# Differential-attention stacks read in two transfers from interleaved maps, with conditioning units, key stacks and loads of heads in other places

## The chip, the cores and the metric

The kernel runs on one core of one Trainium2 chip. The metric is the device time of one execution in microseconds (us); lower is better. In the profile the engines are called PE (TensorE, matrix products), PEld (its weight loads), DVE (VectorE), ACT (ScalarE), POOL (GpSimd) and SP (SyncE, which here issues every transfer between memory and SBUF).

## The reference: what is computed

Two layers over 512 latent tokens and 256 context tokens, model width 1024, batch 1, all in float32. A layer is a token mixer and then a gated convolutional FFN. What the change touches is the first of the mixer's four head groups, differential attention, and the conditioning vectors:

```python
mod_l = (c_act @ w_mod[l] + b_mod[l])[:, None, :]          # conditioning: 6 x 1024 values a layer
hl = modulate(rmsnorm(xl, norm_mix_w[l]), sh1, sc1) @ w_in[l]
q = h[..., :A_Q].reshape(b, s, DIFF_HEADS, 2, DIFF_QK_DIM)  # 4 heads, 2 maps, 32 channels each
s = jnp.einsum('bhiqd,bhikd->bhiqk', q, k).astype(f32) * scale
p = jax.nn.softmax(s, axis=-1)
w = (p[:, :, 0] - lam * p[:, :, 1]).astype(v.dtype)
```

Queries and keys of this group and of the second one (window attention) are turned by a rotary embedding before that.

## The kernel before

**Precision.** Every float32 operand of a product is split into a high and a low part, and products of the parts are added. For the scores of differential attention, one map has 32 channels, so a *stack* of 128 partitions holds four blocks of 32: high, high, low, low for the queries and high, low, high, low for the keys. One product over 128 partitions then gives all four combinations.

**Stages.** A head stage computes the first eight conditioning units (`mod_products`, `mod_sums`; a unit is 256 values, its weights are two loads of 512 KB into tiles `mraw`), the first norm and the first products with `w_in` while its inputs arrive. Then for each layer come the mixer, the output product and the FFN. In the mixer of layer 0, TensorE alternates between pieces of 22 projections with `w_in` (a unit `win`, 512 KB of weights into a tile `raw`, cast by ScalarE into `wh` and reduced by GpSimd to `wl`) and the attention of eight items: A0 heads 0 and 1, A1 heads 0 and 1, B heads 0 and 1, C0, C1. The remaining twelve conditioning units of layer 0 are woven in between the pieces by `side`.

**How a stack comes about.** The projection of queries or keys of a group is turned (`rotate`), split and written to memory by `stash` (tile `qk`, high and low part, 128 channels, 768 tokens). `load` of the group then reads it back as stacks with `stack`: in group A four transfers of 32 partitions each, two stacks (queries and keys) a head. All transfers are issued by SP in the order that the scheduler gives them. `begin` calls `load` at the first score of a head's first item, and for the following head at the first score of its second item (an item is two blocks of 128 queries). Stacks live in a pool `stk` of four buffers. Loads of weights run one unit ahead in layer 0 and two units ahead in layer 1, in a pool of three `raw` buffers that the conditioning weights of the mixer share.

**Order.** The program's order on each engine is what a scheduler made of the code; scores and pieces of TensorE are pinned to the order of the code. Each engine works strictly in its order.

Of the kernel before, what the change touches and what calls it, by code (L numbers as in the profile page):

```python
# [9 lines left out]
F32 = mybir.dt.float32  # L10
# [42 lines left out]
class Trunk:  # L53
# [34 lines left out]
    def build(self):  # L88
# [53 lines left out]
        for j in range(4):  # L142
            for h in (j, j + 4):
                raws = [self.g.tile([128, 2 * T], F32, tag="g", name="mraw") for _ in range(2)]
                raws = [t[:, 0:1024].rearrange("p (g n) -> p g n", g=4) for t in raws]
                for kh in range(2):
                    last = nc.sync.dma_start(out=raws[kh], in_=d["wmod"][h, kh])
                self.mod_sums(0, h, self.mod_products(h, raws, "pj" if h < 4 else "pv"))
            if j == 0:
                self.depth = 0  # L150
                self.prefetch(2)
            ks = range(2 * j, 2 * j + 2)
            self.scale_vec(0, self.amix[0], O_NM, 8, slice(2 * j, 2 * j + 2))
            for sg, rb in zip(SEGS, r):
                self.norm_apply(x, y, sg, self.amix[0], self.mod[0][:, 0:8], rb, ks)
            early = early or self.early_start(0)
            for k in ks:
                for sg in SEGS:
                    self.early_products(early, y, sg, [k])
# [10 lines left out]
        for l in range(DEPTH):  # L170
# [3 lines left out]
            with ExitStack() as es:  # L174
                self.mixing_pools(es)
                todo = []
                if l == 0:
                    todo = list(range(8, 20))
                if l:
                    self.neg_lambda(l)  # L180
                self.mixing(l, y, need, todo)
# [363 lines left out]
    def side(self, last):  # L545
        if self.open:
            self.open.pop()()
        elif self.vq:
            self.vq.pop(0)()
        elif self.todo and not last and self.mraw:  # L550
            h = self.todo.pop(0)
            parts = self.mod_products(h, self.mraw.pop(), "pv" if self.name == "A0" else "tp")
            self.open.append(lambda: self.mod_sums(0, h, parts))
        if self.todo and not self.mraw:
            self.mraw.append(self.mod_load(self.todo[0]))
# [14 lines left out]
    def rotate(self, t, kind):  # L570
        nc = self.nc
        step = 8 if kind == 0 else 16
        mask = [i ^ step for i in range(32)]
        s = self.hl.tile([128, T], F32, tag="hl", name="rot")
# [6 lines left out]
    def split(self, t, NT, vector=False, pool=False):  # L581
# [5 lines left out]
        return hl  # L587

    def stash(self, t, NT, vector=False):

        hl = self.split(t, NT, vector, self.name == "B")
        self.n += 1
        scr = self.tc.dram_tile([2, 128, T], F32, name=f"qk{self.n}")
        self.nc.sync.dma_start(out=scr[:, :, :NT].rearrange("s p t -> p s t"), in_=f32v(hl[:, :, :NT]))
        return scr

    def stack(self, pieces, NT):

        s = self.stk.tile([128, 2, T], F32R, tag="stk", name="stk")
        o = 0  # L600
# [137 lines left out]
    def mixing(self, l, y, need, todo):  # L738
        qs = SEGS if need else SEGS[:1]
        self.l, self.y, self.qs, self.NQ, self.todo = l, y, qs, T if need else SEQ, todo  # L740
        self.open, self.vq, self.later, self.mraw = [], [], [], []
        self.depth = 1 if todo else AHEAD
        self.kept = {}
        self.pairs = []
# [60 lines left out]
        def score(n):  # L805
            nonlocal at
            for _ in range(n):
                if at < len(scores):
# [5 lines left out]
                    after(w * SCORE_SHARE)  # L814

        for n, (name, _, _, ws, v_steps, fin) in enumerate(items):
            v = v_steps()
# [24 lines left out]
    def items(self, g, name, h, need_prep):  # L842
        L = list(g.attend(h))
        for i, (s_steps, ws, v_steps) in enumerate(L):
            yield (name, (lambda i=i: g.begin(h, i, need_prep)) if i in (0, 1) else None, s_steps, ws, v_steps,
                   i == len(L) - 1 and (name[0] != "A" and name[0] != "B" or h == 1))
# [128 lines left out]
class Group:  # L975
# [28 lines left out]

    def k64(self, scr, j):
        src = scr[:, 64 * j:64 * j + 64].rearrange("s d t -> d s t")
        return self.K.stack([src, src], T)


class GroupA(Group):  # L1010
# [7 lines left out]
    def prep(self):  # L1018
        K, P = self.K, self.P
        self.qscr = yield from self.qk(P, self.qs, 32 ** -0.5, 0)  # L1020
        self.kscr = yield from self.qk(2 + P, SEGS, 1.0, 0)
        K.have.add(K.name)
# [4 lines left out]
    def load(self, hh):  # L1027

        self.ops[hh] = [
            self.K.stack([scr[s, 64 * hh:64 * hh + 64, :NT].rearrange("(m d) t -> d m t", d=32) for s in parts], NT)  # L1030
            for scr, parts, NT in ((self.qscr, (0, 0, 1, 1), self.NQ), (self.kscr, (0, 1, 0, 1), T))]

# [84 lines left out]
class GroupB(Group):  # L1117
# [18 lines left out]
    def load(self, j):  # L1136
        self.ops[j] = self.k64(self.kscr, j), self.q64(self.qscr[j])

# [189 lines left out]
def _tables():  # L1328
# [4 lines left out]
    for kind, dim in ((0, 32), (1, 64)):  # L1333
        quarter = dim // 4
        freqs = (f(10000.0) ** (-(np.arange(quarter, dtype=f) / f(quarter)))).astype(f)
        for p in range(128):
            i = p % dim
            pos = rows if i < dim // 2 else cols
# [21 lines left out]
def _layout(i):  # L1360
# [8 lines left out]
    r["wmodt"] = A["w_mod"].reshape(L, D, 48, 128).transpose(0, 2, 3, 1)  # L1369
    r["win"] = A["w_in"].reshape(L, KT, 128, 22, 128).transpose(0, 3, 2, 1, 4)  # L1370
    r["wout"] = A["w_out"].reshape(L, KT, 128, KT, 128).transpose(0, 3, 2, 1, 4)
    r["wup"] = A["ffn_w_up"].reshape(L, KT, 128, 2, NF, 128).transpose(0, 4, 3, 2, 1, 5)
# [39 lines left out]
```

## Time and profile before

| | |
|---|---|
| time, median of 3 runs | 1759.32 us (1756.22 to 1762.36) |
| the profiled execution | 1762.87 us, its span 1761.0 us |
| TensorE busy | 1679.1 us, 95% of the span |
| granted clock of TensorE, mean of the span | 0.986 |
| VectorE, ScalarE, GpSimd busy | 53%, 45%, 58% |
| DMA, mean over the span | 139 GB/s |

TensorE's busy time is the sum of its products, whose ends are modelled; a stretch where it waits is a gap between two rows of its timeline, and the wait's cause stands in brackets at the later row. [...] The time of a transfer has two parts in the profile: how long SP was taken up by issuing it (its row in SP's timeline), and how long it took from issue to landing (the table of DMA issues).

### The profile page before, as it was taken

How to read it: one execution, taken by the hardware profiler on the slowest of the kernel's cores; microseconds unless marked ns; L12 is line 12 of the kernel's file. 1: busy time of each engine (PE TensorE's matmuls, PEld its weight loads, DVE VectorE, ACT ScalarE, POOL GpSimd, SP SyncE). 2: the span in 40 equal slices, each digit the busy share in tenths (PEclk: the TensorE clock that was granted, in tenths of full speed). 3: DMA queues.
4: the chain of work that ended last, by engine and by line, in shares of the span. 5: the costliest groups of instructions: out<-in, count | busy, mean ns of one | idle time of the engine just before them, and what ended most of it. 6: DMA issues, size and time to landing. Idle time of an engine off the chain costs nothing. (4 is left out here: it accounts for less than half of the span.)

```text
span 1761.0 us, 27484 instructions
## 1 busy us (share of the span) xinstructions
PE 1679.1 (95%) x10212; PEld 1448.2 (82%) x10212; DVE 928.5 (53%) x1789; ACT 787.5 (45%) x1355; POOL 1017.3 (58%) x1348
## 2 busy tenths in 40 slices
PE   7899999899999999999999988999999999999997
PEld 4578878798888888888888877888889888888887
DVE  3577767562767644543344566877656522122244
ACT  4377656553533311332133345776654543242343
POOL 1424235766678745775466664424865676676762
PEclk9999999999999999999999999999999999999998
DMA  8675545346533333343334536453436333333334
GB/s 334 177 217 188 156 115 179 93 122 231 168 108 121 124 113 98 120 131 110 119 111 135 181 113 188 138 150 102 147 109 221 106 99 90 102 93 99 96 114 127
DMA packets 78453, 244.21 MB, mean 139 GB/s; under 512 B 9072, under 2 KB 12656, under 8 KB 78192
## 3 DMA queue, kind: packets, MB, share of 16 engines
q1 hardware_dynamic: 78320, 242.46, 43.8%
q8 instruction: 81, 1.33, 0.3%
q14 instruction: 52, 0.43, 0.1%
HBM read 214.64 MB, written 27.79 MB: 138 GB/s over the span
## 5 line engine op out<-in xcount | busy, mean ns | idle before, releaser
L485 POOL TENSOR_TENSOR wl<-raw,wh 128x256 fp32r<-128x256 f32 (+1 forms) x750 | 575.2, 797 | 542.7 <-ACT wh L480 526.5
L480 ACT CAST wh<-raw 128x1024 fp32r<-128x1024 f32 (+1 forms) x228 | 233.5, 1027 | 422.7 <-PE pd L73 194.9
L73 PE MATMUL pu<-yh,wh 128*128 128x512 f32 (+1 forms) x1072 | 377.4, 352 | 1.8 <-DVE up L925 1.8
L73 PE MATMUL pu<-yl,wh 128*128 128x512 f32 (+1 forms) x1072 | 377.2, 352 | 1.8 <-POOL yl L411 1.5
L73 PE MATMUL pu<-yh,wl 128*128 128x512 f32 (+1 forms) x1072 | 376.3, 351 | 0.0
L73 PE MATMUL pd<-g,wh 128*128 128x512 f32 (+1 forms) x1168 | 290.9, 341 | 5.4 <-DVE x L893 2.4
L922 DVE SCALAR_TENSOR_TENSOR up<-pu,par,up 128x511 f32<-128x511 f32 (+1 forms) x132 | 83.0, 657 | 329.0 <-ACT up L920 329.0
L73 PEld LDWEIGHTS pd<-g,wh 128*128 128x128 f32 x1168 | 203.2, 192 | 31.1 <-ACT wh L480 5.6
L73 PEld LDWEIGHTS pu<-yh,wh 128*128 128x128 f32 x1072 | 202.7, 189 | 29.7 <-ACT wh L480 1.5
L73 PEld LDWEIGHTS pu<-yl,wh 128*128 128x128 f32 x1072 | 202.8, 189 | 29.3 <-POOL yl L411 2.1
L73 PEld LDWEIGHTS pu<-yh,wl 128*128 128x128 f32 x1072 | 202.7, 189 | 27.4
L73 PE MATMUL pj<-yh,wh 128*128 128x512 f32 (+1 forms) x608 | 217.4, 361 | 7.2 <-ACT ev L559 4.9
L73 PE MATMUL pj<-yl,wh 128*128 128x512 f32 (+1 forms) x608 | 213.6, 352 | 1.5 <-DVE yl L413 1.4
L73 PE MATMUL pj<-yh,wl 128*128 128x512 f32 (+1 forms) x608 | 212.4, 350 | 0.0
L73 PE MATMUL pd<-g,wl 128*128 128x512 f32 (+1 forms) x584 | 198.4, 341 | 4.6 <-DVE wl L485 4.5
L893 DVE SCALAR_TENSOR_TENSOR x<-pd,mod,x 128x512 f32<-128x512 f32 (+1 forms) x80 | 48.9, 614 | 181.9 <-PE pd L73 181.9
L73 PEld LDWEIGHTS pj<-yh,wh 128*128 128x128 f32 x608 | 117.1, 193 | 26.0 <-ACT ev L559 8.4
L73 PEld LDWEIGHTS pj<-yh,wl 128*128 128x128 f32 x608 | 117.2, 193 | 14.6
L655 POOL TENSOR_TENSOR p<-p,rec 128x512 f32<-128x512 f32 (+2 forms) x80 | 79.5, 997 | 85.6 <-DVE rec L651 62.6
L73 PEld LDWEIGHTS pj<-yl,wh 128*128 128x128 f32 x608 | 117.6, 193 | 13.2 <-DVE yl L413 3.1
L73 PEld LDWEIGHTS pd<-g,wl 128*128 128x128 f32 x584 | 112.3, 192 | 18.0 <-DVE wl L485 5.5
L310 DVE SCALAR_TENSOR_TENSOR junk<-mrow,cbc 128x1024 f32<-128x1024 f32 x80 | 123.2, 1541 | 1.4 <-DMA mrow<-in_wmodt 0.5
(176 smaller groups left out, 2750.5 us busy)
## 6 DMA issues: line engine op xcount, KB each, us to landing
raw<-in_wup SPq DMA_DIRECT2D x88, 512.0 KB, 3.5
mrow<-in_wmodt SPq DMA_DIRECT2D x56, 512.0 KB, 3.8
raw<-in_win SPq DMA_DIRECT2D x44, 512.0 KB, 3.7
raw<-in_wdn SPq DMA_DIRECT2D x48, 448.0 KB, 3.3
mraw<-in_wmod SPq DMA_DIRECT2D x40, 512.0 KB, 7.1
raw<-in_wout SPq DMA_DIRECT2D x32, 512.0 KB, 3.5
qk<-hl SPq DMA_DIRECT2D x16, 768.0 KB, 3.6
stk<-qk SPq DMA_DIRECT2D x32, 384.0 KB, 5.5
```

What stands on the lines that cost most here:

```text
L73: i = self.nc.tensor.matmul(out, **kw)
L310: self.tc.keep_in_program_order(nc.vector.scalar_tensor_tensor(out=junk, in0=raw, scalar=1.0, in1=self.cbc[:, i], op0=ALU.mult, op1=ALU.mu ...
L480: i = nc.scalar.copy(out=wh, in_=raw)
L485: eng.tensor_tensor(out=wl[:, a:b], in0=raw[:, a:b], in1=f32v(wh[:, a:b]), op=ALU.subtract)
L655: self.nc.gpsimd.tensor_tensor(out=p, in0=p, in1=r.broadcast_to(list(p.shape)), op=ALU.mult)
L893: self.nc.vector.scalar_tensor_tensor(out=x[m][:, a:b], in0=p[:, :b - a], scalar=gate[:, m, (0 if b <= SEQ else 1):(1 if b <= SEQ else 2)] ...
L922: nc.vector.scalar_tensor_tensor(out=u[:, a + 1:b], in0=p[:, a:b - 1], scalar=cw[:, 0:1], in1=u[:, a + 1:b], op0=ALU.mult, op1=ALU.add)
```

## The change

Eight edits:

1. The columns of `w_in` for queries and keys of group A are reordered so that the two maps' channels alternate (partition 2d + m holds channel d of map m); the table of the rotary embedding and the shuffle (distance 16 in place of 8) follow it.
2. `stash` writes into a memory tile that is as wide as its tokens, so that the two maps of one channel are one run of memory.
3. A stack of group A is read by `stack2` in two transfers of 64 partitions in place of four of 32. The queries' transfers repeat the high (or low) half with a step of 0; the keys' go over both halves.
4. Of A0's head 0 the query stack is loaded as soon as the queries are stored.
5. A0's head 1 is loaded at the third item of head 0 in place of the second (in layer 1, which has two items, still at the second), pinned to that place in SP's order; B's head 1 likewise at the third item of head 0.
6. The key stack of B's head 1 lives in the pool of the values (`vp`) in place of `stk`.
7. Conditioning units 8 and 9 move from the mixer into the head stage, into its last of four rounds.
8. In the mixer no conditioning weights are loaded and no conditioning unit starts before the first score.

The diff, cut to its core:

```diff
@@ build, head stage
+            more = []
+            if j == 3:
+                for h, tag in ((8, "pj"), (9, "pv")):
+                    raws = [self.g.tile([128, 2 * T], F32, tag="g", name="mraw") for _ in range(2)]
+                    raws = [t[:, 0:1024].rearrange("p (g n) -> p g n", g=4) for t in raws]
+                    for kh in range(2):
+                        nc.sync.dma_start(out=raws[kh], in_=d["wmod"][h, kh])
+                    more.append((h, self.mod_products(h, raws, tag)))
...
-                    todo = list(range(8, 20))
+                    todo = list(range(10, 20))
@@ side
-        elif self.todo and not last and self.mraw:
+        elif self.begun and self.todo and not last and self.mraw:
...
-        if self.todo and not self.mraw:
+        if self.begun and self.todo and not self.mraw:
@@ rotate
-        step = 8 if kind == 0 else 16
-        mask = [i ^ step for i in range(32)]
+        mask = [i ^ 16 for i in range(32)]
@@ stack2 (new), stash
+    def stack2(self, src, same, NT, late=False):
+        s = self.stk.tile([128, 2 * T], F32R, tag="stk", name="stk")
+        for i in range(2):
+            part = src[i:i + 1].broadcast_to([2, 32, 2 * NT]) if same else src
+            self.load(f32v(s[64 * i:64 * i + 64, :2 * NT]), part, late)
+        return s[:, :2 * NT].rearrange("p (m t) -> p m t", m=2)
...
-        scr = self.tc.dram_tile([2, 128, T], F32, name=f"qk{self.n}")
+        scr = self.tc.dram_tile([2, 128, NT], F32, name=f"qk{self.n}")
@@ items
+            second = min(2, len(L) - 1) if (name, h) in (("A0", 0), ("B", 0)) else 1
@@ GroupA
-        self.ops[hh] = [
-            self.K.stack([scr[s, 64 * hh:64 * hh + 64, :NT].rearrange("(m d) t -> d m t", d=32) for s in parts], NT)
-            for scr, parts, NT in ((self.qscr, (0, 0, 1, 1), self.NQ), (self.kscr, (0, 1, 0, 1), T))]
+        have = self.ops.get(hh, [])
+        self.ops[hh] = have + [self.half(hh, i) for i in range(len(have), 2)]
+
+    def half(self, hh, i):
+        scr, NT = (self.kscr, T) if i else (self.qscr, self.NQ)
+        src = scr[:, 64 * hh:64 * hh + 64].rearrange("s (d m) t -> s d (m t)", m=2)
+        return self.K.stack2(src, i == 0, NT, self.P == 0 and hh == 1)
@@ GroupB.load
+        if j:
+            assert sum(K.vlive.values()) < 4
+            K.vlive["B"] += 1
+            home = K.vp
+        self.ops[j] = self.k64(self.kscr, j, home), self.q64(self.qscr[j])
```

What the change does to SP's order shows at three places of layer 0's mixer; each row is one transfer or several equal ones, with its destination, its source and the destination's size. **First place: the start of the mixer**, from the store of A0's queries (`qk_688` before, `qk_728` after) and keys (`qk_701`, `qk_744`) to the stacks of head 0. Before:

```order
L271 DMA mraw<-in_wmod 128x1024
L594 DMA qk_688<-hl_685 128x2x768
L271 DMA mraw<-in_wmod 128x1024
L594 DMA qk_701<-hl_698 128x2x768
L603 DMA stk<-qk_688 32x2x768 x4
L271 DMA mraw<-in_wmod 128x1024 x2
L603 DMA stk<-qk_701 32x2x768 x4
L603 DMA stk<-qk_688 32x2x768 x4
```

After:

```order
L612 DMA qk_728<-hl_725 128x2x768
L612 DMA qk_744<-hl_741 128x2x768
L477 DMA raw<-in_win 128x1024
L477 DMA stk<-qk_728 64x1x1536 x2
L477 DMA stk<-qk_744 64x1x1536 x2
L281 DMA mraw<-in_wmod 128x1024
L612 DMA qk_889<-hl_886 128x2x768
```

The conditioning loads (`mraw`) are gone from among the stores and the stacks, and head 0's stacks are four transfers in place of eight; the query stack still stands behind the store of the keys. **Second place: the loads of A0's head 1 and A1's head 0.** Before, from the store of A1's keys (`qk_1100`) on; A0's head 1 had been loaded earlier, right behind head 0:

```order
L594 DMA qk_1100<-hl_1097 128x2x768
L467 DMA raw<-in_win 128x1024
L1231 DMA rpb<-in_rpb 128x384
L603 DMA stk<-qk_894 32x2x768 x4
L603 DMA stk<-qk_1100 32x2x768 x4
L467 DMA raw<-in_win 128x1024
```

After, from the store of A1's keys (`qk_1056`) on:

```order
L612 DMA qk_1056<-hl_1053 128x2x768
L477 DMA raw<-in_win 128x1024
L477 DMA stk<-qk_728 64x1x1536 x2
L477 DMA stk<-qk_744 64x1x1536 x2
L477 DMA stk<-qk_889 64x1x1536 x2
L477 DMA stk<-qk_1056 64x1x1536 x2
L1265 DMA rpb<-in_rpb 128x384
L477 DMA raw<-in_win 128x1024
```

Eight transfers of stacks, those of two heads, now stand in one row ahead of the next load of weights. **Third place: A1's head 1**, the last load of group A. Before:

```order
L594 DMA qk_1662<-hl_1659 128x2x768
L603 DMA stk<-qk_894 32x2x768 x4
L603 DMA stk<-qk_1100 32x2x768
L467 DMA raw<-in_win 128x1024
L603 DMA stk<-qk_1100 32x2x768 x3
```

After:

```order
L612 DMA qk_1624<-hl_1621 128x2x768
L477 DMA stk<-qk_889 64x1x1536 x2
L477 DMA stk<-qk_1056 64x1x1536 x2
L477 DMA raw<-in_win 128x1024
L281 DMA mraw<-in_wmod 128x1024 x2
```

The load of weights stood among the last of eight transfers and now stands behind all four.

## Rows read from the trace of the kernel before

**Rows 1.** Busy time by stage: head, layer 0's mixer, then to layer 1's mixer.

```profile
core 0: us, PE busy (x) PEld busy (x) DVE busy (x) ACT busy (x) POOL busy (x), PEclk, DMA share, GB/s
20.00:40.00 20.00, 18.09 (x156) 10.65 (x155) 12.41 (x36) 8.83 (x17) 5.53 (x8) 1.00 1.00 405
...
60.00:230.00 170.00, 157.14 (x1009) 129.15 (x1008) 118.77 (x267) 107.99 (x218) 59.61 (x65) 0.98 0.60 184
...
400.00:1060.00 660.00, 649.90 (x3827) 570.97 (x3826) 336.04 (x571) 211.74 (x262) 426.61 (x482) 0.99 0.42 131
1060.00:1185.00 125.00, 116.85 (x675) 100.92 (x674) 94.10 (x166) 84.39 (x151) 49.73 (x60) 0.97 0.53 158
```

**Rows 2.** PE's longest waits at the start of layer 0's mixer: total us, times, longest.

```profile
PE macc L73 <- DMA mraw<-in_wmod: 4.8, 2, 4.5
...
PE sca L73 <- DMA stk<-qk: 1.1, 1, 1.1
```

**Rows 3.** SP's timeline there: start us, us of issuing, line, transfer, count.

```profile
70.33 0.34 SPq L271 DMA_DIRECT2D mraw<-in_wmod  x1
70.71 0.43 SPq L594 DMA_DIRECT2D qk<-hl  x1
71.19 4.28 SPq L603 DMA_DIRECT2D stk<-qk  x4
75.57 1.09 SPq L271 DMA_DIRECT2D mraw<-in_wmod  x2
77.46 6.92 SPq L603 DMA_DIRECT2D stk<-qk  x8
```

**Rows 4.** PE's timeline there: start us, us, tile, count, wait before it.

```profile
75.52 0.74 PE L73 MATMUL macc<-mraw,silc 128*32 128x256 f32 x8 [4.53 <-DMA mraw<-in_wmod]
...
87.80 0.94 PE L73 MATMUL sca<-stk 128*128 128x512 f32 x4 [1.14 <-DMA stk<-qk]
```

**Rows 5.** Two stretches of PE just behind that wait, columns as in Rows 1.

```profile
76.20:79.20 3.00, 3.00 (x12) 2.31 (x9) 0.00 (x0) 1.31 (x2) 1.44 (x3) 0.50 1.09 252
79.60:82.60 3.00, 3.00 (x20) 2.02 (x18) 0.75 (x5) 0.30 (x1) 0.95 (x2) 1.00 1.02 352
```

**Rows 6.** DMA issues: transfer, count, KB each, median us from issue to landing.

```profile
raw<-in_win SPq DMA_DIRECT2D x44, 512.0 KB, 3.7
...
stk<-qk SPq DMA_DIRECT2D x32, 384.0 KB, 5.5
stk<-qk SPq DMA_DIRECT2D x48, 192.0 KB, 5.5
...
out<-ot SPq DMA_DIRECT2D x8, 256.0 KB, 2.1
```

**Rows 7.** PE's timeline: first scores of A0 head 1, A1 heads 0 and 1.

```profile
118.94 0.51 PE L73 MATMUL sca<-stk 128*128 128x512 f32 x2
...
155.36 0.59 PE L73 MATMUL sca<-stk 128*128 128x512 f32 x2
...
193.14 0.39 PE L73 MATMUL sca<-stk 128*128 128x512 f32 x1
```

**Rows 8.** SP's timeline: A1's key store, then three loads of weights of units.

```profile
109.49 0.38 SPq L594 DMA_DIRECT2D qk<-hl  x1
112.19 0.33 SPq L467 DMA_DIRECT2D raw<-in_win  x1
...
128.09 0.35 SPq L467 DMA_DIRECT2D raw<-in_win  x1
...
157.06 1.58 SPq L467 DMA_DIRECT2D raw<-in_win  x1
```

**Rows 9.** ACT's casts of the last two of those, PE's first products with them.

```profile
138.15 1.03 ACT L480 CAST wh<-raw 128x1024 fp32r<-128x1024 f32 x1
146.98 0.50 PE L73 MATMUL pj<-yh,wh 128*128 128x512 f32 x1
147.31 0.40 PE L73 MATMUL pj<-yl,wh 128*128 128x512 f32 x1
147.55 0.39 PE L73 MATMUL pj<-yh,wl 128*128 128x512 f32 x1
...
164.14 1.05 ACT L480 CAST wh<-raw 128x1024 fp32r<-128x1024 f32 x1
173.73 0.39 PE L73 MATMUL pj<-yh,wh 128*128 128x512 f32 x1
```

**Rows 10.** SP and PE at the start of layer 1's mixer.

```profile
1070.23 6.49 SPq L603 DMA_DIRECT2D stk<-qk  x10
...
1079.62 0.59 PE L73 MATMUL sca<-stk 128*128 128x512 f32 x2 [1.16 <-DMA stk<-qk]
...
1100.59 0.52 PE L73 MATMUL sca<-stk 128*128 128x512 f32 x2
```

**Rows 11.** PE's timeline: scores of group C that waited for stacks.

```profile
324.46 0.71 PE L73 MATMUL scc<-stk 128*128 128x256 f32 x4 [2.81 <-DMA stk<-qk]
...
1278.75 1.19 PE L73 MATMUL scc<-stk 128*128 128x256 f32 x4 [3.31 <-DMA stk<-qk]
```

More of the change, by code (lines that the diff above doesn't have):

```diff
@@ L155, in build @@
                 self.norm_apply(x, y, sg, self.amix[0], self.mod[0][:, 0:8], rb, ks)
+            for h, parts in more:
+                self.mod_sums(0, h, parts)
             early = early or self.early_start(0)
@@ L592, in stash, with stack @@
         self.n += 1
-        scr = self.tc.dram_tile([2, 128, T], F32, name=f"qk{self.n}")
-        self.nc.sync.dma_start(out=scr[:, :, :NT].rearrange("s p t -> p s t"), in_=f32v(hl[:, :, :NT]))
-        return scr
-    def stack(self, pieces, NT):
-        s = self.stk.tile([128, 2, T], F32R, tag="stk", name="stk")
+        scr = self.tc.dram_tile([2, 128, NT], F32, name=f"qk{self.n}")
+        self.nc.sync.dma_start(out=scr.rearrange("s p t -> p s t"), in_=f32v(hl[:, :, :NT]))
+        return scr
+    def stack(self, pieces, NT, home=None):
+        s = (home or self.stk).tile([128, 2, T], F32R, tag="v" if home else "stk", name="stk")
         o = 0
@@ L742, in mixing @@
         self.depth = 1 if todo else AHEAD
+        self.begun = False
         self.kept = {}
@@ L814, in score @@
                     after(w * SCORE_SHARE)
+            self.begun = self.begun or n > 0
         for n, (name, _, _, ws, v_steps, fin) in enumerate(items):
@@ L844, in items @@
         for i, (s_steps, ws, v_steps) in enumerate(L):
-            yield (name, (lambda i=i: g.begin(h, i, need_prep)) if i in (0, 1) else None, s_steps, ws, v_steps,
+            second = min(2, len(L) - 1) if (name, h) in (("A0", 0), ("B", 0)) else 1
+            yield (name, (lambda i=i: g.begin(h, i, need_prep)) if i in (0, second) else None, s_steps, ws, v_steps,
                    i == len(L) - 1 and (name[0] != "A" and name[0] != "B" or h == 1))
@@ L1003, in q64, with k64 @@
         return self.K.stack([scr[s, :, :self.NQ].rearrange("(g d) t -> d g t", d=64) for s in range(2)], self.NQ)
-    def k64(self, scr, j):
+    def k64(self, scr, j, home=None):
         src = scr[:, 64 * j:64 * j + 64].rearrange("s d t -> d s t")
-        return self.K.stack([src, src], T)
+        return self.K.stack([src, src], T, home)
 class GroupA(Group):
@@ L1020, in prep @@
         self.qscr = yield from self.qk(P, self.qs, 32 ** -0.5, 0)
+        if P == 0:
+            self.ops[0] = [self.half(0, 0)]
         self.kscr = yield from self.qk(2 + P, SEGS, 1.0, 0)
@@ L1136, in load @@
     def load(self, j):
-        self.ops[j] = self.k64(self.kscr, j), self.q64(self.qscr[j])
+        K = self.K
+        home = None
+        if j:
[3 more added lines that the diff above has]
+        self.ops[j] = self.k64(self.kscr, j, home), self.q64(self.qscr[j])
     def attend(self, j):
@@ L1336, in _tables @@
         for p in range(128):
-            i = p % dim
+            i = p % 64 // 2 if kind == 0 else p % dim
             pos = rows if i < dim // 2 else cols
@@ L1370, in _layout @@
     r["win"] = A["w_in"].reshape(L, KT, 128, 22, 128).transpose(0, 3, 2, 1, 4)
+    two = np.arange(128).reshape(2, 2, 32).transpose(0, 2, 1).reshape(128)
+    r["win"] = np.concatenate([r["win"][:, :4][..., two], r["win"][:, 4:]], axis=1)
     r["wout"] = A["w_out"].reshape(L, KT, 128, KT, 128).transpose(0, 3, 2, 1, 4)
```

## The prediction

> **What bounds the kernel now.** I read the stages first: in the FFN TensorE is busy 649.9 of 660 us, in layer 0's differential attention 157.1 of 170 and in layer 1's 116.9 of 125 [rows 1]. The change touches nothing of the FFN, so all it can save lies in these gaps; what it can lose has no such limit, since TensorE works in order and waits for whatever it needs next. I then read whom TensorE waits for where the change acts: at the start of layer 0's mixer 4.5 us for conditioning weights and 1.1 us for head 0's stacks [rows 2, 4]. SP's timeline gives the reason: the weights' load is issued at 70.33, the keys' store and four stack transfers right behind it, and SP is taken up 4.28 us by those four and 6.92 us by the next eight [rows 3]; the load lands at 75.5 among this traffic. [...] Last come group C's scores, which wait 2.81 us in layer 0 and up to 3.31 us in layer 1 for stacks that found no free buffer [rows 11].
>
> **The change part by part.**
>
> *Free edits.* The reordered columns, the rotary table and the shuffle's distance change no count and no size of an instruction. The width of the stored tile changes addresses alone.
>
> *Conditioning units.* Twenty units stay twenty; two of them move. What goes away is the wait of 4.5 us, and the 1.1 us for stacks if these come sooner. Behind the wait, 3 us at half clock did half the work [rows 5]; with the stretch's whole length a little over 3 us, some 1.6 us come back. Gain: 7 us. The cover of what is moved is the head stage, where from 20 to 40 us the DMA engines are busy all the time at 405 GB/s [rows 1]: the four added loads of 512 KB are 2.1 MB, 5.2 us at that rate. The loads of three units' weights stand behind them. Bounds: 0, if the quiet stretch from 40 us on takes them, and 5.2 us. I take 1 us, since the first of these weights is wanted only when the products of the first two units are done.
>
> *Key stack of B in the values' pool.* A1 and B leave `stk` a buffer sooner, so C0's second key stack can be loaded with the first. Gain between 0 and 2.81 us in layer 0 and 0 and 3.31 in layer 1 [rows 11]; I take 4 us together.
>
> *Two transfers for four.* This is the edit that decides. Before, a stack of 768 KB is four transfers of 192 KB whose source leads with 32 channels; others, of 384 KB, lead with 64. Both kinds land in 5.5 us [rows 6], and every other transfer leads with 128. The new source leads with the two halves (or with a step of 0, twice), then 32 channels, then one run of 6,144 bytes. No row shows a transfer whose source leads with so few entries, so its cost has two ends. If the 64 runs are dealt to all 16 DMA engines, the nearest row in bytes holds (384 KB, 5.5 us), and SP issues two instructions for four. If the engines are dealt whole leading entries, there are two to deal, and two engines carry everything. An engine moves 405/16 = 25.3 GB/s when all are busy [rows 1]. A transfer of 393,216 bytes then takes 7.8 us, a stack 15.5, a head 31; in layer 1, with 512 queries (262,144 bytes), a head takes 26 us. Everything else on SP's queue has a sixteenth of its bytes on each of the two engines and arrives only after the stacks ahead of it. I take this end: what all known sources share is a leading count that 16 divides, and that is the property that the edit removes; how close the new transfer is in bytes says nothing on how it is dealt out. It is a choice, not a reading.
>
> [...]
>
> *The walk of layer 0 at that end.* I add 2 us from a transfer's last byte to its use (a lone 256 KB store lands in 2.1 us, a 512 KB load in 3.7 [rows 6]).
> - A0 head 0. The loads still stand behind the keys' store, and before they start at 71.2 [rows 3]. 71.2 + 31 + 2 = 104; the first score was at 87.8 [rows 4]. **+16.**
> - A0 head 1. Its loads now stand behind A1's key store and one load of weights, which before came at 109.5 and 112.2 [rows 8], 22 to 24 us after the first score; the pieces run a little earlier now, so 20 us: 104 + 20 = 124, and 124 + 31 + 2 = 157. Before, head 1 starts 31 us after head 0 [rows 4, 7]; the new order of TensorE has 29 more rows of products between the two, which follow each other by up to 0.24 us [rows 9], some 5 us. Wanted at 140. **+17.**
> - The next load of weights stands behind this head's and A1 head 0's transfers, 62 us on the two engines: 124 + 62 + 2 = 188. Before, that load was issued at 128.1 and cast at 138.15 [rows 8, 9], 19 us after head 1's first score, and its products began 9 us later at 146.98. With the 5 us from above they want it at 157 + 14 + 9 = 180; it is cast at 190. **+10.**
> - A1 head 0 is there at 188 and wanted at 157 + 31 + 10 = 198. Nothing.
> - A1 head 1 is loaded when head 1's buffers come free, at 198, and there at 231; the load of weights behind it is at 232, cast at 234. Before, that unit's products began at 173.73 [rows 9], 18 us after A1 head 0's first score [rows 7]: wanted at 216. **+18.** A1 head 1 itself was wanted 38 us after head 0 [rows 7], at 236 plus this wait: nothing.
>
> Layer 0: +61 us.
>
> *Layer 1.* The loads start at 1070.2 [rows 10]: 1070.2 + 26 + 2 = 1098, first score before 1079.6, **+18.** Head 1 follows at once, there at 1124, wanted 21 us after head 0 [rows 10], at 1119: **+5.** Weights are loaded two units ahead here, so I allow only **+5** for A1. Layer 1: +28.
>
> *Clock.* The wait of 4.5 us cost some 1.6 us of clock behind it. Six waits of 5 us or more, less two such stretches that fall away: +6 us. The other side is that DVE and ACT catch up in the long waits, and small waits behind them go: −4 us.
>
> *Sum.* The walk starts from the old first score, so the 7 us of the start are in it already. 61 + 28 + 6 − 4 (catching up) + 1 (head stage) − 4 (group C) = +88 us. The profiled execution took 1762.9 us, which gives 1851; it was 3.6 us above the median of the runs shown, so **1847 us** against the median 1759.3. The terms are waits in a row in which each shifts the next, so its own range is wide: with only the waits at the three first loads (16 + 17 + 18 − 4) 1806, and if units later in the group also wait, as much again as a third of the walk, 1880. I take 1800 to 1885.
>
> **The rivals.**
>
> *Spread over all engines, and faster.* Against two engines: both old kinds of transfers go at 5.5 us. Then the gains stand alone: 7 + 4 − 1 = 10 us, **1749 us**, bounds 1741 (all of C's waits, no loss at the head) and 1754. It decides as soon as the runs are dealt one by one.
>
> *Spread, and given back.* The 2.1 MB at the head cost their 5.2 us because the early products and the weights queue behind them, and C's stacks wait for something else: 7 − 5.2 = 2 us, **1757 us**, no measurable change.
>
> *Two engines, but hidden.* Loads run a head ahead, and a head lasts 31 to 38 us [rows 4, 7] against 31 us of loading. If SP issued each head's loads a whole head earlier and the weights had their slack, only the first loads would show: 16 + 18 us less 8, **1785 us**. Against it: in the new order A0's head 1 is loaded behind A1's keys, some 16 us before its use, and weights have 7 to 10 us from load to cast [rows 8, 9].
>
> **How the numbers follow.** Two engines with most waits open 0.62, hidden for the most part 0.10, spread and faster 0.21, spread and given back 0.07. About 0.3% (5 us) is what a measurement of this kernel can tell from no change. Slower takes the first two: 0.72. Faster: 0.21. The same: 0.07. The likeliest is 1847 us. Its own range with the hidden case is 1780 to 1885 and holds 0.7; to leave out no more than 0.2, the range must reach into the spread cases: **1746 to 1885 us**.
>
> **What the profile of the changed kernel would show.** [...] Spread: 5 us or less to landing, first score at about 82 us, no wait over 3 us for stacks, and the wait for conditioning weights gone in both cases. The head stage shows its own term: the first product of the third unit at its old time, or up to 5 us later. I am wrong in size rather than kind if weights prove to have more slack than the two casts show; wrong in kind if the landings are short.

## The result and the profile after

The change made the kernel slower: 1904.09 us (median of 6 runs, 1899.89 to 1910.12) against 1759.06 us of the kernel before (6 runs), a ratio of 1.0827 with a 95% interval of 1.081 to 1.0845. The prediction had the direction and the mechanism, but 1847 us, and its range ended at 1885. Of all the runs below, one of experiment 10's twelve was in a slower state (1955.81 us at a mean clock of 0.80); its ratio leaves that run out. The profiled execution's span is 1898.0 us against 1761.0; TensorE's busy time grew from 1679.1 to 1688.6 us, so of the 137 us between the spans 127.5 are time in which TensorE stands idle and 9.5 are slower products.

First the stages of the kernel after, as in [rows 1]: layer 0's mixer up to group B's first score, the stretch from its output product to the next mixer, and group A of layer 1 (the wait of 21.5 us at its start begins at 1174.7 and so lies in both of the last two).

```profile
core 0: us, PE busy (x) PEld busy (x) DVE busy (x) ACT busy (x) POOL busy (x), PEclk, DMA share, GB/s
...
60.00:328.00 268.00, 161.74 (x958) 135.33 (x957) 116.04 (x251) 106.83 (x215) 55.71 (x64) 0.80 0.32 106
500.00:1180.00 680.00, 662.20 (x3887) 581.67 (x3885) 344.39 (x582) 216.54 (x269) 439.98 (x498) 0.99 0.42 131
1180.00:1324.00 144.00, 105.65 (x578) 91.65 (x579) 81.13 (x146) 76.77 (x138) 35.45 (x43) 0.84 0.33 110
```

TensorE works 161.7 of 268 us where it worked 157.1 of 170, and the DMA engines, which have to carry what it waits for, are busy only a third of the time. TensorE's timeline names the waits of layer 0 (the first four) and four of layer 1:

```profile
107.92 1.62 PE L73 MATMUL sca<-stk 128*128 128x512 f32 x4 [29.40 <-DMA stk<-qk]
...
173.38 0.98 PE L73 MATMUL sca<-stk 128*128 128x512 f32 x2 [23.52 <-DMA stk<-qk]
...
208.33 0.80 PE L73 MATMUL pv<-wth,va 128*128 128x256 f32 x2 [16.80 <-ACT wth L743]
...
265.12 1.01 PE L73 MATMUL sca<-stk 128*128 128x512 f32 x2 [26.82 <-ACT p L661]
...
1196.25 1.62 PE L73 MATMUL sca<-stk 128*128 128x512 f32 x4 [21.52 <-DMA stk<-qk]
...
1224.47 0.98 PE L73 MATMUL sca<-stk 128*128 128x512 f32 x2 [4.34 <-issue]
...
1256.97 0.98 PE L73 MATMUL sca<-stk 128*128 128x512 f32 x2 [3.36 <-issue]
...
1287.62 0.58 PE L73 MATMUL pj<-yh,wh 128*128 128x256 f32 x1 [12.53 <-ACT ev L569]
```

Two of layer 0's waits end with ScalarE, not with a transfer. ScalarE's timeline shows what held it: a cast of weights that had not landed, with what TensorE wanted queued behind it (at 206.75 `wth`, the second operand of `pv`, at 263.13 the exponentials `p`).

```profile
134.71 1.05 ACT L490 CAST wh<-raw 128x1024 fp32r<-128x1024 f32 x1
...
206.75 1.04 ACT L490 CAST wh<-raw 128x1024 fp32r<-128x1024 f32 x1 [16.62 <-DMA raw<-in_win]
...
263.13 1.04 ACT L490 CAST wh<-raw 128x1024 fp32r<-128x1024 f32 x1 [29.75 <-DMA raw<-in_win]
264.09 0.90 ACT L661 ACTIVATE p<-sca,nm 128x768 f32<-128x768 f32 x1
...
1286.45 0.62 ACT L593 CAST hl<-ev 128x512 fp32r<-128x512 f32 x1 [12.84 <-DMA qk<-hl]
```

SP's timeline shows what stood ahead of those weights. Eight stack transfers now take SP 38.51 us to issue, where eight took 6.92 before [rows 3], and each load of weights goes out behind them:

```profile
71.25 10.06 SPq L477 DMA_DIRECT2D stk<-qk  x4
...
138.67 0.33 SPq L477 DMA_DIRECT2D raw<-in_win  x1
139.05 38.51 SPq L477 DMA_DIRECT2D stk<-qk  x8
177.66 7.02 SPq L1265 DMA_DIRECT2D rpb<-in_rpb  x1
184.78 1.52 SPq L477 DMA_DIRECT2D raw<-in_win  x1
...
223.94 7.63 SPq L477 DMA_DIRECT2D stk<-qk  x4
231.69 0.36 SPq L477 DMA_DIRECT2D raw<-in_win  x1
```

Last, stretches in which nothing but stacks moves (83 to 87 and 160 to 170 us), and what follows the first wait, columns as in the first group:

```profile
83.00:87.00 4.00, 0.00 (x0) 0.00 (x0) 0.00 (x0) 0.00 (x0) 0.00 (x0) 0.50 0.13 54
108.00:112.00 4.00, 4.00 (x11) 3.23 (x12) 1.82 (x2) 2.02 (x2) 0.00 (x0) 0.50 0.09 35
112.00:116.00 4.00, 4.00 (x17) 3.24 (x16) 2.23 (x5) 2.11 (x5) 0.00 (x0) 0.84 0.41 164
...
160.00:170.00 10.00, 0.00 (x0) 0.00 (x0) 0.00 (x0) 0.00 (x0) 0.00 (x0) 0.50 0.13 53
```

A DMA share of 0.13 is two of sixteen engines (0.125), and 53 GB/s is 26.5 for each. This one column points at the mechanism; experiments 1 and 5 test it. The table of DMA issues, whose landings were to decide, gives none for the stacks of this run; the share of a quiet stretch does the same service.

### The profile page after: what moved, and what is told of

It is laid out like the page before. It is cut to its first block, busy times and chain, and to the rows that moved or that the text cites. A ratio compares the mean times of both kernels' runs of the same rounds, so it can differ in the third digit from the quotient of the medians.

```text
span 1898.0 us, 27442 instructions
## 1 busy us (share of the span) xinstructions
PE 1688.6 (89%) x10212; PEld 1455.6 (77%) x10212; DVE 924.5 (49%) x1785; ACT 788.1 (42%) x1355; POOL 1013.0 (53%) x1348
## 5 line engine op out<-in xcount | busy, mean ns | idle before, releaser
L73 PE MATMUL sca<-stk 128*128 128x256 f32 (+1 forms) x144 | 44.3, 391 | 110.6 <-DMA stk<-qk 74.4
L73 PEld LDWEIGHTS pj<-yh,wl 128*128 128x128 f32 x608 | 120.4, 198 | 14.8
```

What stands on the lines that cost most here:

```text
L73: i = self.nc.tensor.matmul(out, **kw)
```

## The experiments

Three theories stood for the loss. **First:** the DMA engines are dealt whole leading entries of a transfer, and two of them are all there is to deal. **Second:** something else of the new transfers is slow (the repeated read with a step of 0, the runs of 6,144 bytes, 64 partitions at once). **Third:** the other edits, 4 to 8, which move loads and units.

**1. The channel leads.** The kernel after with the same transfers, bytes, runs and order, but the 32 channels first in the source:

```diff
-        src = scr[:, 64 * hh:64 * hh + 64].rearrange("s (d m) t -> s d (m t)", m=2)
+        src = scr[:, 64 * hh:64 * hh + 64].rearrange("s (d m) t -> d s (m t)", m=2)
...
-            part = src[i:i + 1].broadcast_to([2, 32, 2 * NT]) if same else src
+            part = src[:, i:i + 1].broadcast_to([32, 2, 2 * NT]) if same else src
```

> The changed kernel with one thing different: the source of each of the two transfers names the 32 channels first and the two halves second, so it leads with 32 entries; the partitions of both stacks follow that order. Bytes, runs of 6,144 bytes, the repeated read with a step of 0, 64 partitions, count of transfers and the order of instructions on every engine stay. Theory 1 (engines are dealt whole leading entries, two of them): the waits for stacks go, first score of layer 0 at 78 to 84 us, time 1735 to 1757 us. Theory 2 (the repeated read, the long runs or the 64 partitions make the transfer slow): 1890 us or more, as in the changed kernel. Theory 3 (the other edits, which moved loads and conditioning units, cost the time): also 1890 us or more.

Measured: 1753.24 us, ratio 0.9971 (0.9961 to 0.9982). The whole loss is gone with one exchange of two dimensions. The second theory falls as far as the repeated read, the runs and the number of partitions go, since all three are unchanged, and the third falls with it, since edits 4 to 8 are all still there.

**2. Four transfers of 32 partitions.** Again the kernel after, with the transfers' old number and the new layout:

```diff
-        for i in range(2):
-            part = src[i:i + 1].broadcast_to([2, 32, 2 * NT]) if same else src
-            self.load(f32v(s[64 * i:64 * i + 64, :2 * NT]), part, late)
+        for i in range(4):
+            part = src[i // 2 if same else i % 2]
+            self.load(f32v(s[32 * i:32 * i + 32, :2 * NT]), part, late)
```

> The changed kernel with each stack read in four transfers of 32 partitions, each leading with 32 channels, runs of 6,144 bytes; all other edits stay. Theory 1: 1738 to 1760 us, within 5 us of the run in which the channels lead, the difference being SP's time to issue twice the transfers. Theory 2: the same if the repeated read or the 64 partitions are slow. Theory 3: 1890 us or more.

Measured: 1754.22 us, 0.9977 (0.9966 to 0.9988). As the run before it: two or four transfers make no difference by themselves.

**3. The two transfers alone.** The kernel before with edits 1 to 3 and nothing else:

```diff
+            self.K.stack2(scr[:, 64 * hh:64 * hh + 64].rearrange("s (d m) t -> s d (m t)", m=2), i == 0, NT)
+            for i, (scr, NT) in enumerate(((self.qscr, self.NQ), (self.kscr, T)))]
```

> The kernel before with edits 1 to 3 alone (interleaved maps, width of the stored tile, two transfers for a stack whose source leads with the two halves); conditioning units, key stack of B and the places of loads as before. Theory 1: 1840 to 1900 us; head 1's loads stand right behind head 0's, so the wait for head 1 should be small and the weights behind both should wait instead. Theory 3: 1755 to 1765 us.

Measured: 1905.7 us, 1.0844 (1.0817 to 1.087). Edits 1 to 3 hold the whole loss, 5.7 us over the expected range. As expected, no wait for head 1's stacks shows in layer 0; TensorE waits there for conditioning weights (41.5 us in three waits) and behind ScalarE for exponentials (48.4 us in three) in its place.

**4. Queries alone.** The kernel after with the queries' stacks as they are and the keys' in four transfers of 32 partitions:

```diff
-        for i in range(2):
+        for i in range(2 if same else 4):
+            n = 64 if same else 32
...
-            part = src[i:i + 1].broadcast_to([2, 32, 2 * NT]) if same else src
+            part = src[i:i + 1].broadcast_to([2, 32, 2 * NT]) if same else src[i % 2]
```

> The changed kernel in which only the queries' stacks take two transfers that lead with the two halves (the repeated read); the keys' take four transfers of 32 partitions that lead with 32. Theory 1: half the bytes on two engines, a head 15.5 us in place of 31 in layer 0 and 10.4 in place of 26 in layer 1; first score at about 88 us, time 1780 to 1820 us. Theory 2 in the form that the repeated read alone is slow: 1890 us or more. In the form that only the keys' transfers are slow: 1740 to 1760 us.

Measured: 1820.97 us, 1.0355 (1.0327 to 1.0382). Less than half of the loss for half of the stacks: 62 us over the kernel before on that chip (1758.9 us), against 147 in experiment 3. That is 1 us over the expected range, and the first score of layer 0 comes at 97.5 us, not at about 88.

**5. Four and eight leading entries.** Experiment 2 with the 32 channels renumbered, alike in queries and keys, so that the source leads with 4 (then 8), and the same with 8 (then 4):

```diff
             part = src[i // 2 if same else i % 2]
+            part = part.rearrange("(a b) t -> b a t", b=4)
```

> As the run with four transfers of 32 partitions, but their source is renumbered so that it leads with 4 entries (then 8, then a run of 6,144 bytes); queries and keys are permuted alike, so the scores are the same sums. If the engines are dealt out by the leading entries, four engines carry a stack: 4/16 = 0.25 of DMA share while stacks alone move, about 106 GB/s (twice the 53 GB/s of the changed kernel), a stack of 768 KB in 7.8 us in place of 15.5, the first score of layer 0 at 87 to 95 us in place of 107.9, 1765 to 1800 us. If the number of leading entries does not matter, it is as with 32 of them: 1754 us, the first score at about 83 us.

> The same with 8 leading entries (then 4, then a run of 6,144 bytes). Dealt out by leading entries: a DMA share of 0.5 while stacks alone move, about 210 GB/s. That is about what transfers of 64 partitions reach on all 16 engines (199 to 237 GB/s), so hardly anything is lost: 1753 to 1760 us. If the loss comes from any lead under 16, it is as slow as four leading entries or slower.

Measured: 1789.03 us, 1.0175 (1.0161 to 1.0189) with four, and 1760.95 us, 1.0021 (1.0009 to 1.0033) with eight, a microsecond over its expected range. The stretch in which stacks move alone, with four:

```profile
74.00:76.00 2.00, 1.31 (x8) 0.85 (x8) 0.66 (x2) 0.60 (x1) 0.15 (x1) 1.00 0.25 101
76.00:78.00 2.00, 2.00 (x19) 2.00 (x19) 0.78 (x3) 0.00 (x0) 1.80 (x1) 1.00 0.25 104
```

With eight:

```profile
76.00:78.00 2.00, 1.98 (x16) 1.98 (x17) 1.42 (x3) 0.00 (x0) 1.18 (x1) 1.00 0.50 190
```

The share is k/16 with k leading entries, three times over: 0.13, 0.25, 0.50, at 53 to 54, 101 to 104 and 190 GB/s. With 32 leading entries it is 0.97 to 1.05 (experiment 1, windows in experiment 8). The first theory is shown for these counts; a count that neither divides 16 nor is a multiple of it was not run.

| leading entries | ratio to before | first score of layer 0, us | first score of group B, us |
|---|---|---|---|
| 2 (after) | 1.0827 | 107.9 | 328.2 |
| 4 (experiment 5) | 1.0175 | 90.4 | 252.6 |
| 8 (experiment 5) | 1.0021 | 84.6 | 231.2 |
| 32 (experiment 2) | 0.9977 | 82.9 | 229.6 |
| 32 (before, other edits absent) | 1 | 87.8 | 229.0 |

**6. Head 1 of A0 early.** The prediction's walk put that head's loads at 124 us; they went out at 139. Here edit 5 is undone for A0:

```diff
-            second = min(2, len(L) - 1) if (name, h) in (("A0", 0), ("B", 0)) else 1
+            second = min(2, len(L) - 1) if (name, h) == ("B", 0) else 1
...
-        return self.K.stack2(src, i == 0, NT, self.P == 0 and hh == 1)
+        return self.K.stack2(src, i == 0, NT)
```

> The changed kernel (two leading entries) with edit 5 undone for A0: head 1's four transfers are issued right behind head 0's and are not pinned. The step in question is where head 1's loads stand: in the changed kernel they went out at 139 us, behind a load of weights that waited for a free buffer. Here head 1's stacks should be there at about 140 us and its wait of 23.5 us go down to 0 to 4 us. Theory (two engines carry every stack, and all that is issued behind them pays): the weights and stores issued behind both heads' transfers land after 135 us, so the time comes back as waits of ScalarE for weights ahead of the next products, and the total stays at 1885 to 1905 us. Rival (the place of these loads decided the size of the loss): 1870 to 1883 us.

Measured: 1891.95 us, 1.0767 (1.075 to 1.0783). The 23.5 us for head 1's stacks are gone, but a wait for conditioning weights takes the larger part of their place, and the two behind ScalarE stay. TensorE's timeline:

```profile
140.74 1.08 PE L73 MATMUL macc<-mraw,silc 128*32 128x256 f32 x8 [14.52 <-DMA mraw<-in_wmod]
...
198.38 1.01 PE L73 MATMUL sca<-stk 128*128 128x512 f32 x2 [14.37 <-ACT p L661]
...
256.85 1.01 PE L73 MATMUL sca<-stk 128*128 128x512 f32 x2 [27.59 <-ACT p L661]
```

ScalarE's, just ahead of the last two:

```profile
196.40 1.04 ACT L490 CAST wh<-raw 128x1024 fp32r<-128x1024 f32 x1 [15.47 <-DMA raw<-in_win]
...
254.86 1.04 ACT L490 CAST wh<-raw 128x1024 fp32r<-128x1024 f32 x1 [30.49 <-DMA raw<-in_win]
```

Where the stacks stand decides who waits for them, and hardly how much: the ratio fell by 0.006, some 11 us of 145.

**7. What the other edits are worth.** Both runs start from experiment 1. One takes back edits 7 and 8 (the conditioning units), the other edit 6 (B's key stack in the values' pool):

```diff
-            if j == 3:
+            if False:
...
-                    todo = list(range(10, 20))
+                    todo = list(range(8, 20))
...
-        self.begun = False
+        self.begun = True
```

> The kernel with the channels leading (1753.2 us), with edits 7 and 8 undone: units 8 and 9 are back in the mixer, and conditioning weights are loaded from its start. Theory: at the start of layer 0 one wait only took the place of the other (4.5 us for conditioning weights before, 5.4 us for stacks behind the edits), so undoing them changes nothing: 1751 to 1756 us, with the wait for conditioning weights of 3 to 5 us back and the first score at 84 to 89 us. Rival: the two edits are what gains; then it is 1757 to 1761 us.

```diff
-        if j:
-            assert sum(K.vlive.values()) < 4
-            K.vlive["B"] += 1
-            home = K.vp
```

> The kernel with the channels leading, with edit 6 undone: B's head 1 has its key stack in the pool of the stacks again. Theory: the gain of that kernel lies in group C, whose scores found their stacks late for want of a buffer; without edit 6 these waits return (2 to 4 us from the first score of C to the output product in each layer), 1756 to 1760 us. Rival: edit 6 does nothing, 1752 to 1755 us.

Measured: without edits 7 and 8 1753.95 us, 0.9978 (0.9969 to 0.9988), the same as with them; without edit 6 1759.42 us, 1.0004 (0.9995 to 1.0012). So edits 7 and 8 are worth nothing that this shows, and edit 6 some 0.33%, 6 us. Why the first is so: with those edits the wait for conditioning weights goes, but TensorE then waits for head 0's stacks and is slower behind it: products of 512 columns start 0.43 us apart from 84.85 to 88.69 us, as they do at a granted 0.50 from 109 to 112 us in the kernel after, and 0.23 us apart from 89 us on. Its first score does come earlier (83.43 us against 88.94), but with 522 rows of products ahead of it in place of 538; group B then has 628 rows in place of 609, and group C's first score comes at 323.23 and 323.36 us, level. TensorE's timeline of experiment 1:

```profile
83.43 1.62 PE L73 MATMUL sca<-stk 128*128 128x512 f32 x4 [5.45 <-DMA stk<-qk]
```

The waits of TensorE without edits 7 and 8, then without edit 6, then in experiment 1 (total us, times, longest):

```profile
PE macc L73 <- DMA mraw<-in_wmod: 4.8, 1, 4.8
```

```profile
PE scc L73 <- DMA stk<-qk: 7.0, 3, 2.8
```

```profile
PE scc L73 <- DMA stk<-qk: 2.7, 1, 2.7
```

Without edit 6 group C waits three times for its stacks, with it once. From its first score to the output product it takes 1.8 us longer in layer 0 and 2.1 in layer 1, 3.9 of the 6 us; where the rest goes is open.

**8. Even and odd partitions.** In experiment 1 all sixteen engines are busy while stacks move, and still only some 200 to 240 GB/s arrive, against 405 with transfers to 128 partitions [rows 1]. Its windows, at the start of layer 0 and at the loads of two heads later on:

```profile
78.00:80.00 2.00, 0.00 (x0) 0.00 (x0) 0.18 (x1) 1.21 (x2) 0.00 (x0) 1.00 1.00 221
80.00:82.00 2.00, 0.00 (x0) 0.00 (x0) 0.00 (x0) 0.00 (x0) 0.00 (x0) 1.00 0.97 199
...
119.00:121.00 2.00, 2.00 (x13) 1.74 (x12) 1.29 (x2) 0.85 (x2) 0.00 (x0) 1.00 1.00 221
121.00:123.00 2.00, 2.00 (x13) 1.72 (x12) 0.00 (x0) 0.11 (x1) 0.00 (x0) 1.00 1.05 230
123.00:125.00 2.00, 2.00 (x11) 1.62 (x10) 0.85 (x2) 1.44 (x3) 0.00 (x0) 1.00 0.99 215
```

Either the range of 64 neighbouring partitions holds them, or something of their reads. So the two transfers of a stack go to every second partition in place of the lower and the upper half (the repeated read moves from the queries' stack to the keys'):

```diff
-            part = src[:, i:i + 1].broadcast_to([32, 2, 2 * NT]) if same else src
-            self.load(f32v(s[64 * i:64 * i + 64, :2 * NT]), part, late)
+            part = src if same else src[:, i:i + 1].broadcast_to([32, 2, 2 * NT])
+            self.load(f32v(s[i::2, :2 * NT]), part, late)
```

> The kernel with the channels leading (1753.2 us), but the two transfers of a stack of group A go to the even and to the odd partitions, in place of the lower and the upper 64; both stacks are permuted alike, so the scores are the same sums. The transfers to 64 neighbouring partitions moved 199 to 237 GB/s at a DMA share of 1.00, those to 128 partitions 416 GB/s. If the narrow range of partitions is what holds them, the even or odd 64 go at 300 GB/s or more, the first score's wait of 5.4 us shrinks by 2 to 4 us, and the time is 1747 to 1752 us. If it is something else of these transfers (their reads of memory, their runs of 6,144 bytes), the rate stays at 200 to 240 GB/s and the time at 1752 to 1755 us.

Measured: 1749.73 us, 0.9956 (0.9941 to 0.9972). The windows at the same two heads, whose transfers go out from 108.18 us on here and from 114.57 us on in experiment 1, and TensorE's first score:

```profile
112.00:114.00 2.00, 2.00 (x16) 1.86 (x15) 0.99 (x2) 1.07 (x2) 0.00 (x0) 1.00 0.94 344
114.00:116.00 2.00, 2.00 (x11) 1.67 (x10) 0.30 (x1) 0.00 (x0) 0.00 (x0) 1.00 1.01 396
116.00:118.00 2.00, 2.00 (x13) 1.72 (x13) 0.61 (x2) 0.95 (x3) 0.00 (x0) 1.00 1.03 426
```

```profile
77.91 0.94 PE L73 MATMUL sca<-stk 128*128 128x512 f32 x4 [0.97 <-DMA stk<-qk]
```

Same bytes, same runs, as many repeated reads: 344 to 426 GB/s in place of 215 to 230, and the wait of 5.45 us is 0.97. The range of partitions was the limit of the rate in experiment 1; why 64 neighbouring ones take no more than 199 to 230 GB/s is not shown. The gain in time over experiment 1 is not shown by this run, since the two intervals overlap; that of experiment 9 lies clear of experiment 1's.

**9. All stacks so.** The stacks of the other groups in the same way:

```diff
-        o = 0
-        for src in pieces:
-            n = src.shape[0]
-            self.nc.sync.dma_start(out=f32v(s[o:o + n, :, :NT]), in_=src)
-            o += n
+        for o, src in enumerate(pieces):
+            self.nc.sync.dma_start(out=f32v(s[o::len(pieces), :, :NT]), in_=src)
```

> The same with the stacks of the other groups too (two transfers each, to the even and to the odd partitions). If the narrow range is what holds them, group C's waits for stacks (2.7 us and less) shrink as well: 1744 to 1751 us. If not, as the run before it.

Measured: 1744.58 us, 0.9928 (0.9915 to 0.9941), the fastest of all. Its interval touches that of experiment 8, and the two spans are 1743.3 and 1744.4 us, so what the other groups add stays open; that it beats both kernels does not.

**10. That edit alone.** The kernel before with the same edit of `stack`, none of edits 1 to 8:

> The kernel before with one edit: piece number o of a stack of n pieces is written to every n-th partition, from o on, in place of a block of neighbours; nothing of edits 1 to 8. (The scheduler puts a few loads elsewhere for it, and in layer 1 some pieces of the projections ahead of the first scores.) If the narrow range of partitions is what slows the transfers of stacks and this is what the last two runs gained, 1748 to 1754 us, with stacks in layer 0 there sooner and a shorter wait for conditioning weights. If the gain needs the edits too (two transfers in place of four, B's key stack elsewhere), 1755 to 1760 us.

Measured: 1751.44 us, 0.996 (0.9946 to 0.9974). The stacks' rows in the table of DMA issues, then TensorE's longest wait:

```profile
stk<-qk SPq DMA_DIRECT2D x32, 384.0 KB, 4.2
stk<-qk SPq DMA_DIRECT2D x48, 192.0 KB, 3.7
```

```profile
PE macc L73 <- DMA mraw<-in_wmod: 5.4, 1, 5.4
```

Both kinds landed in 5.5 us before [rows 6]. The wait for conditioning weights that I expected to shrink did not (4.8 us in two waits before [rows 2]). Nor does the first score come sooner (91.0 us against 87.8), though it no longer waits for stacks. The gain lies in group C instead, which takes 69.0 us from its first score to the output product against 73.7 in layer 1, and 78.4 against 80.6 in layer 0. Some loads and, in layer 1, pieces of projections stand elsewhere in this program, so a part may be due to that.

## Why the prediction was right in kind and wrong in size

**Two engines.** Right, and shown (experiments 1, 3 and 5). I took this end, as a choice, because 16 divides every leading count that the old trace showed; the leading count turned out to be the property that counts. What the rows gave for its price held too: 25.3 GB/s an engine forecast, 26.5 measured; 31 us for a head's stacks and 2 to their use, and head 1's first score came 34.3 us after the issue at 139.05.

**The walk.** This is what failed: 61 us for layer 0 and 28 for layer 1 forecast, 99 and 44.5 measured. The loss of each term is the time from one first score to the next, less the same distance before ([rows 4, 7]; A1's two heads start at 224.6 and 292.3 us after). The forecast's 17 and 10 for A0 head 1 and A1 head 0 are waits; as distances they are 22 and 5, since the 29 rows of products (5 us) that the walk saw join the first distance leave the second. They did move: TensorE's rows in these two distances, before and then after, columns as in the first group:

```profile
87.80:118.94 31.14, 28.38 (x178) 23.21 (x179) 24.17 (x55) 22.82 (x45) 7.90 (x9) 1.00 0.72 228
118.94:155.36 36.42, 36.07 (x238) 30.26 (x237) 29.17 (x67) 26.15 (x54) 16.36 (x14) 1.00 0.53 174
```

```profile
107.92:173.38 65.46, 38.25 (x212) 32.16 (x212) 27.05 (x57) 26.23 (x51) 10.04 (x13) 0.79 0.24 90
173.38:224.58 51.20, 33.46 (x202) 27.49 (x202) 24.80 (x60) 23.27 (x47) 11.11 (x10) 0.79 0.38 126
```

| term | forecast | measured |
|---|---|---|
| A0 head 0's first score | +16 | +20.1 |
| from there to A0 head 1 | +22 | +34.3 |
| from there to A1 head 0 (weights) | +5 | +14.8 |
| from there to A1 head 1 (weights) | +18 | +29.9 |
| from there to group B | 0 | +0.1 |
| layer 1: head 0 | +18 | +17.1 |
| layer 1: the rest of group A | +10 | +27.4 |
| groups B and C, both layers | −4 | −6.0 |

The measured terms add up to 137.7 us, of which the rest of layer 1 gives 0.7 back; the forecast ones add up to 85, or 88 with the clock's +6, the head stage's +1 and −4 for what catches up. The clock has no row of its own, because slower products sit inside the measured distances. The other 8 us of the 145 between the medians are the profiled executions: before 3.8 us over its median (1762.87 against 1759.06), after 4.2 us under it (1899.89 against 1904.09). Four steps failed.

*When head 1's loads go out.* I wrote "the pieces run a little earlier now, so 20 us: 104 + 20 = 124". They went out at 139.05, 31.1 us after the first score, which is 11 of the 12 us missing in that row. Before, the load of weights ahead of them went out 24.4 us after it [rows 4, 8], and 6.4 us later now. That load waits for a buffer that an earlier unit's cast (at 134.71) and reduction free, and there are 142 rows of products up to that load in place of 126, at a lower clock: 0.50 from 108 to 112 us and 0.84 up to 116, then 0.85 and 0.80 in the two stretches of 5 us from 120 to 130, all at 1.00 before. By these shares up to 4.4 of the 6.4 us are the clock's, an estimate, since TensorE did not work all of that time; the 16 more rows come on top. I had the clock as one term for the whole kernel (+6); it belonged in the walk, since it also makes the next loads late.

*When the weights are wanted.* I counted 9 us of slack from the cast to the products. Most of it is not there. ScalarE works in order, and the exponentials of the next scores stand behind the cast: `p` at 264.09 follows the cast at 263.13, and TensorE's wait ends at 265.12. Once ScalarE stood before a cast (from 190.13 and from 233.38), TensorE went on for 1.4 and 4.9 us and then stopped (191.53 and 238.30). For the first of the two casts I had put the need 23 us (14 + 9) after A0 head 1's first score; ScalarE was ready for it 16.8 us after. For the second, ScalarE was ready at 233.38 (263.13 − 29.75), 8.8 us after A1 head 0's first score. Before, it made the cast 8.8 us after that score as well (164.14 − 155.36 [rows 7, 9]), and I had put the need at 18 us. The step that says what is queued behind the waiting instruction was done for SP and TensorE, not for ScalarE.

*The stores.* In layer 1 ScalarE waits 12.84 us at 1286.45, because the store of an earlier `hl` is still on its way: it is issued at 1259.6, behind four stack transfers. The walk has no store in it, and "only **+5** for A1" rested on the weights alone. The store costs TensorE the 12.53 us at 1287.62; two more waits ahead of scores, 4.34 and 3.36 us, have no cause in the profile that I can name, so a part of the 27.4 stays open.

*The first loads.* 36.7 us from issue to first score in place of 33. From 75 to 79 us 37 GB/s moved and from 79 to 83 us 45, before the 54 of the next stretch; why is not shown.

Experiment 6 shows that these steps are not independent prices: with head 1's loads early the wait of 23.5 us goes, one of 14.5 us comes, and the two behind ScalarE's casts are 14.4 and 27.6 us in place of 16.8 and 26.8.

**The conditioning units.** Their price in the head stage can't be read: the last product of the first eight units starts at 47.85 us after and at 46.52 before, but at 47.76, 47.80 and 48.38 in experiments 3, 7 (without edits 7 and 8) and 10, which add no unit to the head. That +1 looks right is no evidence. The gain of 7 us was wrong even for the kernel whose stacks are spread: experiment 7 finds nothing, because a wait for the next transfer took most of the freed place and the products that the earlier first score skips follow in group B. Only with faster stacks does the first score come at 77.9 us with a wait under 1 us.

**Groups B and C.** Right in direction, and near in size by luck. In the profile group C gains 1.7 us in layer 0 and 6.4 in layer 1, and group B loses 2.1 in layer 0, where it has 18 more rows of products. I had priced the waits alone; in layer 1 TensorE's busy time in group C fell from 66.4 to 61.8 us, so 4.5 of the 6.4 are products at a higher clock (0.91 before, 1.00 after).

**The rivals.** With the transfers spread, experiment 1 measures 1753.2 us, between "Spread, and faster" (1749 us, bounds 1741 and 1754) and "Spread, and given back" (1757 us): group C's gain came, the conditioning units' did not. "Two engines, but hidden" fell: A1's stacks were there in time in layer 0, but the weights behind them were not.

## What to carry to other kernels

Read a transfer's access pattern by its slowest dimension before its bytes: here 32 leading entries kept all sixteen DMA engines busy (a share of 0.97 to 1.05), and 2, 4 and 8 gave 0.13, 0.25 and 0.50, which a stretch where one kind of transfer moves alone shows at once. So put the long dimension first, and treat a step of 0 or a pair of halves as the second one. Slow transfers on SP's queue were paid for by what stood behind them, weights (casts that waited 16.62 and 29.75 us) and a store (12.84 us), and data was wanted as soon as the first engine that touches it had other work queued behind (the exponentials at 264.09 us behind the cast at 263.13), not only when a product used it. Where all engines are busy and half the rate arrives (199 to 230 GB/s here, against 344 to 426), look at the destination's partitions: interleaving the transfers of a stack over them gained 0.4% here as one edit of the kernel before, and the kernel that has it and the sound parts of this change is 0.7% faster than before.

## What was not expected of the hardware

That destination partitions set the rate to such a degree had not been in the forecast: with a DMA share of about 1 (0.94 to 1.05), 199 to 230 GB/s into 64 neighbouring partitions and 344 to 426 GB/s into every second one. It may also be why eight leading entries lose so little (0.50 of the engines, 190 GB/s in experiment 5): 64 neighbouring partitions took hardly more (199 to 230 GB/s) with all sixteen. No run shows that, since experiment 5's transfers go to 32 partitions each.
